# An embedding projection as split float32r products, and the last head's transposes two units later

## The chip, the cores and the metric

The kernel runs on one core of a Trainium2 chip. The metric is the device time of one execution, in microseconds (us), as the median of several runs. TensorE is called PE, with its weight loads as PEld; VectorE is DVE, ScalarE is ACT, GpSimd is POOL, SyncE is SP. SP, ACT and POOL also issue transfers (DMAs), each in its own order.

## The reference

One step of a one-layer decoder, for 512 prompt rows and 64 sample rows (576 rows in all, here split into two halves of 288 columns). All inputs are float32.

```python
def finish_layer(x, attn, conv_y, pe, g_attn_out, w_out, g_mlp, w_up, w_down, g_ple, w_ple, w_ple_gate):
    B, L = x.shape[0], x.shape[1]
    attn = rms_norm(attn, g_attn_out.reshape(N_HEADS, HEAD_DIM)).reshape(B, L, ATT_WIDTH)
    x = x + jnp.concatenate([attn, conv_y], axis=-1) @ w_out
    hid = jnp.square(jax.nn.relu(rms_norm(x, g_mlp) @ w_up))
    x = x + hid @ w_down
    gate = jax.nn.sigmoid(rms_norm(x, g_ple) @ w_ple_gate)
    return x + (pe @ w_ple) * gate
```

Ahead of this stand the input projection (q, k, v, forget gates and the convolution's inputs), attention of the prompt rows over themselves, attention of the sample rows over a paged cache of 2048 rows, and a causal convolution. The change concerns `pe @ w_ple`: `pe` is 576 x 256, `w_ple` 256 x 2048.

## The kernel before, in words

Everything is kept transposed: features lie on the 128 partitions, the 576 rows along the free dimension. A matmul's weights are a 128x128 block, its moving operand 288 columns.

Most products are made in three parts. A float32 operand is split into a high part of type float32r (ACT, `split_hi`, a copy that rounds) and the low rest (DVE, `split_lo`, operand minus high part). The product is then high x high + high x low + low x high. `mm6` issues this for one 128x128 block of weights: three parts for each of two halves of the rows, six matmuls into one accumulator `U` of PSUM. There are two accumulators U, and the tile allocator decides which one a new tile gets.

Phase 1 runs the input projection tile by tile (`gemm_tile`), and `half` is called between half chunks of it. There it takes one step each from queues of generators: convolution and the end of sample attention (`side`), the prompt heads (`att`, `prompt_head`), sample attention (`decode`). Each engine carries out its instructions in the order in which the program issues them.

When sample attention is through, the pool `mid` is opened, and `ple_loads` issues the loads of `pe` (tile `praw`) and of the first weights of `w_ple` (tile `wple`) from POOL. When the input projection is through, a loop drains the rest: per round two units of the embedding projection (`ple`), each followed by one step of the last prompt head, then one step of what is left of sample attention (`fq`), and one step of `out_rows`, which loads a pair of 128-row blocks of the attention result (`rp<-am`, from SP) and splits it into `xh[j]`, `xl[j]` for the output projection. Pairs 0 to 5 are built in the rounds; pairs 6 and 7, which hold the last heads, are loaded after all units and multiplied last in each tile of the output projection (`OUT_ORDER`).

A unit of `ple` makes 128 of the 2048 output features: plain float32 matmuls for two blocks of weights and two halves of rows, into one U. ACT (even units) or DVE (odd units) copies U into the tile `plt`, and SP stores it to `pl` in HBM, two units to a store. The weights come in four pieces of 512 KB, with two buffers, `praw` has a buffer of its own.

A step of the prompt head is: scores of a block of 128 queries, transposes of the probabilities (`turned`), product with the values (`values`). After the last `values`, a chain of twelve small DVE operations (`rsqrt`) normalizes the head's output `o`, PE transposes `o` (four transposes into `T`), ACT copies `T` to `amt`, and POOL stores it to `am`. While the input projection runs, two empty steps stand ahead of those transposes; during the drain there are none:

```python
        if not self.draining:
            for _ in range(2):
                yield
```

The units of the drain are numbered 0 to 15 here. Phase 2 (output projection's end, MLP, gate, final norm) follows behind and is not touched.

Of the kernel before, what the change touches and what calls it, by code (L numbers as in the profile page):

```python
# [9 lines left out]
F32 = mybir.dt.float32  # L10
F32R = mybir.dt.float32r
I32 = mybir.dt.int32
AF = mybir.ActivationFunctionType
# [132 lines left out]
class Kern:  # L146
# [102 lines left out]
    def phase1(self):  # L249
# [105 lines left out]
        nc.gpsimd.memset(f(self.cb), 0.0)  # L355


        side, att, fq = deque(), deque(), deque()
# [98 lines left out]
        assert D["mid"] is not None  # L457
        self.draining = True
        fq.extend(side)
        ple = self.ple(D["mid"])  # L460
        rows = self.out_rows(D["mid"])
        next(rows)
# [260 lines left out]
    def prompt_head(self, h, hb):  # L723
# [64 lines left out]
        for qt in range(4):  # L788
# [9 lines left out]
                self.rsqrt(sm, rs, ss, [128, 4], "h")  # L798
                nc.vector.tensor_tensor(o, o, rs[:, :, None].broadcast_to([128, 4, 128]), ALU.mult)
            yield  # L800
        if not self.draining:
            for _ in range(2):
                yield
        t = self.T_()
        for qt in range(4):
            nc.tensor.transpose(t[:, qt * 128:qt * 128 + 128], o[:, qt, :], self.ident)
# [304 lines left out]


    def ple_loads(self, mid):
        nc, a = self.nc, self.a
        self.pp = mid.tile([128, 2, NR], F32, name="praw", tag="p", bufs=1)
        nc.gpsimd.dma_start(self.pp, a["p"])
        self.wple = {}
        for e in range(2):
            self.ple_weights(mid, e)

    def ple_weights(self, mid, e):
        if e < 4:
            self.wple[e] = mid.tile([128, 8, 128], F32, name="wple", tag="wple")
            self.nc.gpsimd.dma_start(self.wple[e], self.a["w_ple"][e])

    def ple(self, mid):
        nc = self.nc
        for e in range(8):
            pr = mid.tile([128, 2, NR], F32, name="plt", tag="plt")
            w = self.wple[e // 2]  # L1130
            for n in range(2):
                u = self.U_()
                for kt in range(2):
                    for r in range(2):
                        nc.tensor.matmul(u[:, r, :HR], w[:, 4 * (e % 2) + 2 * n + kt, :], self.pp[:, kt, r * HR:(r + 1) * HR],
                                         start=(kt == 0), stop=(kt == 1))
                out = pr[:, n, :].rearrange("p (a b) -> p a b", a=2)
                if n:
                    nc.vector.tensor_copy(out, u[:, :, :HR])
                    nc.sync.dma_start(self.pl[e], pr)  # L1140
                    if e % 2:
                        self.ple_weights(mid, e // 2 + 2)
                else:
                    nc.scalar.activation(out, u[:, :, :HR], AF.Copy)
                yield


    def out_rows(self, mid):
# [737 lines left out]
def layout(inp):  # L1886
# [17 lines left out]
    d["w_ple"] = C(g["w_ple"][0].reshape(2, 128, 4, 4, 128).transpose(2, 1, 3, 0, 4).reshape(4, 128, 8, 128))  # L1904
# [56 lines left out]
```

## Time and profile before

| | |
|---|---|
| median of 3 runs | 2700.09 us (2697.12, 2700.09, 2708.5) |
| profiled execution | 2699.89 us |
| its span | 2698.1 us |
| granted clock of PE, mean | 0.996 |
| drain, first unit to first product of the output projection | 769.42 to 810.69 us |
| PE busy in the span | 98% |

The span is what the trace covers; the execution's own time is 1.8 us longer. In the rows of the trace a plain float32 matmul of the program shows as two records, a float32r matmul as one. A row in order of time gives its start, its length, engine, line, operation, what is written from what, the number of merged instructions, and in brackets the idle time of the engine just before with what ended it.

### The profile page before, as it was taken

Reading aid. Unit: us, or ns where it says so; the run is one execution under the profiler, and the core shown is the slowest. Engines: PE = TensorE matmul, PEld = TensorE weight load, DVE = VectorE, ACT = ScalarE, POOL = GpSimd, SP = SyncE. Lnnn points to the kernel's source line nnn. Section 1 sums busy time; section 2 is a strip of 40 time slices with the busy share of each in tenths; the row PEclk is TensorE's granted clock in tenths of the full one; section 3 lists DMA queues with packets and bytes.
Section 4 is the critical chain, followed back from the end, with each engine's and each line's share of the span. In section 5 each row is a group of like instructions: output and inputs, shape, how many; then the busy total and the mean of one; then the engine's idle time right before and its main releaser. Section 6 shows DMA issues by size and latency. Waiting matters only on the chain. (4 is left out here: it accounts for less than half of the span.)

```text
span 2698.1 us, 56355 instructions
## 1 busy us (share of the span) xinstructions
PE 2648.6 (98%) x21873; PEld 2561.3 (95%) x21873; DVE 2044.6 (76%) x3557; ACT 1160.0 (43%) x1704; POOL 517.3 (19%) x915
## 2 busy tenths in 40 slices
PE   9999999999999999999999999999999999999997
PEld 8899989888989999999999999999999999999997
DVE  6577777656554458888988888798888888888676
ACT  5222232335443335445544444454444444444554
POOL 2288786711000000001100000110000000000110
PEclk9999999999999999999999999999999999999999
DMA  5598888899755554445544444676565655656575
GB/s 204 174 303 295 292 295 289 294 308 321 260 191 162 173 195 161 156 142 165 165 144 141 138 146 142 237 204 186 166 186 153 182 163 172 181 174 219 185 240 168
DMA packets 240110, 544.38 MB, mean 202 GB/s; under 512 B 25729, under 2 KB 26754, under 8 KB 239842
## 3 DMA queue, kind: packets, MB, share of 16 engines
q1 hardware_dynamic: 171410, 330.95, 38.2%
q0 software_dynamic: 34896, 148.86, 17.4%
q10 hardware_dynamic: 33536, 60.96, 6.9%
q8 instruction: 171, 2.80, 0.4%
q14 instruction: 97, 0.79, 0.1%
HBM read 445.60 MB, written 95.09 MB: 200 GB/s over the span
## 5 line engine op out<-in xcount | busy, mean ns | idle before, releaser
L1607 PE MATMUL P<-xs,w2h 128*128 128x288 f32 x3584 | 1062.9, 297 | 8.1 <-DVE c L1726 3.8
L1608 PE MATMUL P<-xs,w2h 128*128 128x288 f32 x3584 | 1061.5, 296 | 2.0 <-DVE xs L155 2.0
L1609 PE MATMUL P<-xs,w2l 128*128 128x288 f32 x3584 | 1058.5, 295 | 2.5 <-DVE w2l L155 2.5
L152 ACT ACTIVATE w2h<-w2r 128x896 fp32r<-128x896 f32 (+1 forms) x632 | 560.3, 891 | 773.2 <-PE P L1608 459.1
L155 DVE TENSOR_TENSOR w2l<-w2r,w2h 128x896 fp32r<-128x896 f32 (+1 forms) x632 | 638.3, 1012 | 217.6 <-ACT w2h L152 215.5
L1607 PEld LDWEIGHTS P<-xs,w2h 128*128 128x128 f32 x3584 | 675.2, 188 | 14.1 <-DVE c L1726 7.0
L1608 PEld LDWEIGHTS P<-xs,w2h 128*128 128x128 f32 x3584 | 675.8, 189 | 3.4 <-DVE xs L155 3.2
L1609 PEld LDWEIGHTS P<-xs,w2l 128*128 128x128 f32 x3584 | 673.8, 188 | 3.9 <-DVE w2l L155 3.9
L498 PE MATMUL U<-xh,whi 128*128 128x288 f32 x1792 | 397.7, 303 | 0.1
L498 PE MATMUL U<-xl,whi 128*128 128x288 f32 x1792 | 381.4, 294 | 0.9 <-DVE xl L337 0.9
L498 PE MATMUL U<-xh,wlo 128*128 128x288 f32 x1792 | 381.7, 294 | 0.0
L498 PEld LDWEIGHTS U<-xh,whi 128*128 128x128 f32 x1792 | 285.9, 188 | 18.8 <-issue 16.3
L126 ACT ACTIVATE whi<-wraw 128x512 fp32r<-128x512 f32 x224 | 140.7, 629 | 355.1 <-PE U L498 295.2
L498 PEld LDWEIGHTS U<-xl,whi 128*128 128x128 f32 x1792 | 287.0, 188 | 1.8 <-DVE xl L337 1.7
L498 PEld LDWEIGHTS U<-xh,wlo 128*128 128x128 f32 x1792 | 286.9, 188 | 0.0
L132 DVE TENSOR_TENSOR wlo<-wraw,whi 128x512 fp32r<-128x512 f32 x224 | 158.3, 708 | 115.0 <-ACT whi L126 114.4
L1045 DVE SCALAR_TENSOR_TENSOR y<-ue,cv,y 128x512 f32<-128x512 f32 x240 | 184.7, 769 | 5.3
L1832 DVE TENSOR_TENSOR w2r<-w2r 128x512 f32<-128x512 f32 (+1 forms) x273 | 178.0, 652 | 5.1 <-DMA w2r<-in_w_down 5.1
L1046 POOL TENSOR_SCALAR cvt<-us,cv 128x64 f32<-128x64 f32 x240 | 165.4, 689 | 22.3
L1679 PE MATMUL P<-xs,w2l 128*128 128x288 f32 x512 | 151.6, 296 | 1.0 <-DVE w2l L155 0.9
L1677 PE MATMUL P<-xs,w2h 128*128 128x288 f32 x512 | 152.0, 297 | 0.0
L1678 PE MATMUL P<-xs,w2h 128*128 128x288 f32 x512 | 151.4, 296 | 0.0
(390 smaller groups left out, 2772.5 us busy)
## 6 DMA issues: line engine op xcount, KB each, us to landing
k<-in_cache_kv SPq DMA_DIRECT2D x256, 256.0 KB, 4.7
v<-in_cache_kv SPq DMA_DIRECT2D x256, 256.0 KB, 4.9
w2r<-in_w_up SPq DMA_DIRECT2D x127, 512.0 KB, 4.0
w2r<-in_w_down SPq DMA_DIRECT2D x112, 512.0 KB, 4.2
wraw<-in_w_main ACTq DMA_DIRECT2D x156, 256.0 KB, 5.0
xs<-di POOLq DMA_DIRECT2D x32, 1008.0 KB, 6.1
w2r<-in_w_gate SPq DMA_DIRECT2D x60, 512.0 KB, 4.5
x<-c POOLq DMA_DIRECT2D x48, 576.0 KB, 6.0
```

The source lines that it names most:

```text
L132: self.nc.vector.tensor_tensor(lo, self.raw.pop(c), f(hi), ALU.subtract)
L152: self.nc.scalar.activation(out, in_, AF.Copy, **kw)
L155: self.nc.vector.tensor_tensor(out, in_, f(hi), ALU.subtract)
L498: self.nc.tensor.matmul(u[:, r, :HR], w, x[:, r * HR:(r + 1) * HR], start=first and n == 0, stop=last and n == 2)
L1045: nc.vector.scalar_tensor_tensor(y, ue[:, j:j + NPR], w, y, ALU.mult, ALU.add)
L1046: nc.gpsimd.tensor_scalar(t, us[:, :, j:j + 8], w, None, ALU.mult)
L1607: nc.tensor.matmul(o, hi[:, ia, :], s.hi[:, ib, :], start=(i == 0), stop=False)
L1608: nc.tensor.matmul(o, hi[:, ia, :], s.lo[:, ib, :], start=False, stop=False)
L1609: nc.tensor.matmul(o, lo[:, ia, :], s.hi[:, ib, :], start=False, stop=(i == n - 1))
L1677: nc.tensor.matmul(o, hi[:, ia, :], s.hi[:, kh, rows], start=first and kh == 0, stop=False)
L1679: nc.tensor.matmul(o, lo[:, ia, :], s.hi[:, kh, rows], start=False, stop=last and kh == 1)
L1832: lambda: V(w[:, :, 4:6, :], w[:, :, 0:1, :].broadcast_to([128, m, 2, 128]), w[:, :, 1:3, :], ALU.add),
```

## The change

The embedding projection is made of split products. The input `praw` is split once into `px` (high and low). The weights come in eight pieces of 256 KB with three buffers, and are split unit by unit into `wph` (ACT) and `wpl` (DVE), two units ahead of their products. Input and the first two units are split by `ple_ahead`, a generator that `half` steps before the drain. `praw` now takes one of the two buffers of `rp`. Each unit has a `plt` of its own (three buffers) and its own store of 288 KB. The two empty steps ahead of the last head's transposes are now taken during the drain also.

```diff
+            step(pq)
...
+                    pq.append(self.ple_ahead(D["mid"]))
...
-        if not self.draining:
-            for _ in range(2):
-                yield
+        for _ in range(2 if self.draining else 2):
+            yield
...
+        self.praw = mid.tile([128, 2, NR], F32, name="praw", tag="rp")
+        self.nc.gpsimd.dma_start(self.praw, self.a["p"])
+        self.pl_x = mid.tile([128, 2, 2, NR], F32R, name="px", tag="px", bufs=1)
+        self.wple, self.units = {}, {}
+        for e in range(3):
             self.ple_weights(mid, e)
 
     def ple_weights(self, mid, e):
-        if e < 4:
-            self.wple[e] = mid.tile([128, 8, 128], F32, name="wple", tag="wple")
+        if e < 8:
+            self.wple[e] = mid.tile([128, 4, 128], F32, name="wple", tag="wple", bufs=3)
             self.nc.gpsimd.dma_start(self.wple[e], self.a["w_ple"][e])
+
+    def ple_unit(self, mid, u):
+        if u < 16:
+            e, n = u // 2, u % 2
+            hi, lo = (mid.tile([128, 2, 128], F32R, name=x, tag=x, bufs=3) for x in ("wph", "wpl"))
+            w = self.wple[e][:, 2 * n:2 * n + 2, :]
+            self.split_hi(hi, w)
+            self.split_lo(lo, w, hi)
+            self.units[u] = hi, lo
+            if n:
+                self.ple_weights(mid, e + 3)
+
+    def ple_ahead(self, mid):
+        for _ in range(4):
+            yield
+        for kt in range(2):
+            hi, lo, x = self.pl_x[:, 0, kt, :], self.pl_x[:, 1, kt, :], self.praw[:, kt, :]
+            self.split_hi(hi, x)
+            self.split_lo(lo, x, hi)
+            yield
+        for u in range(2):
+            self.ple_unit(mid, u)
+            yield
 
     def ple(self, mid):
         nc = self.nc
-        for e in range(8):
-            pr = mid.tile([128, 2, NR], F32, name="plt", tag="plt")
-            w = self.wple[e // 2]
-            for n in range(2):
-                u = self.U_()
-                for kt in range(2):
-                    for r in range(2):
-                        nc.tensor.matmul(u[:, r, :HR], w[:, 4 * (e % 2) + 2 * n + kt, :], self.pp[:, kt, r * HR:(r + 1) * HR],
-                                         start=(kt == 0), stop=(kt == 1))
...
+        xh, xl = self.pl_x[:, 0], self.pl_x[:, 1]
+        for i in range(16):
+            u = self.U_()
+            self.ple_unit(mid, i + 2)
+            hi, lo = self.units.pop(i)
+            for kt in range(2):
+                self.mm6(u, hi[:, kt, :], lo[:, kt, :], xh[:, kt, :], xl[:, kt, :], kt == 0, kt == 1)
+            t = mid.tile([128, NR], F32, name="plt", tag="plt", bufs=3)
+            out = t.rearrange("p (a b) -> p a b", a=2)
+            if i % 2:
+                nc.vector.tensor_copy(out, u[:, :, :HR])
+            else:
+                nc.scalar.activation(out, u[:, :, :HR], AF.Copy)
+            nc.sync.dma_start(self.pl[i // 2][:, i % 2, :], t)
+            yield
```

How the change stands in the engines' order is seen best at the end of the drain. PE before, from the head's last values (`S<-vn,pT`) over unit 11, the transposes (`T<-ident,o`) and units 12 to 15 to the output projection:

```order
L758 MATMUL S<-vn,pT 128x128 x4
L1135 MATMUL U<-praw,wple 128x288 x4
L806 MATMUL T<-ident,o 128x128 x4
L1135 MATMUL U<-praw,wple 128x288 x16
L498 MATMUL U<-xh_195,whi 128x288 x2
```

PE now, from the end of unit 12 (`U_12155`) over unit 13 (`U_12175`) and the transposes to the start of unit 14 (`U_12205`), with the engines whose signals an instruction waits for:

```order
L502 MATMUL U_12155<-px_11486,wpl_12093 128x288 x2
L502 MATMUL U_12175<-px_11486,wph_12134 128x288 [waits Activation_49]
L502 MATMUL U_12175<-px_11486,wph_12134 128x288 x3
L502 MATMUL U_12175<-px_11486,wpl_12135 128x288 [waits DVE_49]
L502 MATMUL U_12175<-px_11486,wpl_12135 128x288
L502 MATMUL U_12175<-px_11486,wph_12134 128x288 x4
L502 MATMUL U_12175<-px_11486,wpl_12135 128x288 x2
L809 MATMUL T_12195<-ident_156,o_11690 128x128 x4
L502 MATMUL U_12205<-px_11486,wph_12156 128x288 [waits DVE_49]
```

The transposes have moved behind units 12 and 13; they wait for nothing of their own any more, and unit 13 ahead of them waits for ACT at its first product and for DVE at its first product with `wpl`.

ACT before, from the split of row pair 3 (`xh_201`) over the copy of unit 10, the head's last output `o` with its squares, and the copy of the transposes (`amt`), to the copies of units 12 and 14 and pair 5:

```order
L152 ACTIVATE xh_201<-rp 128x1152
L1144 ACTIVATE plt<-U 128x576
L761 ACTIVATE o<-S,l_11686 128x128
L762 ACTIVATE S,ss<-S,l_11686 128x128
L808 ACTIVATE amt<-T,gat 128x512
L152 ACTIVATE xh_203<-rp 128x1152
L1144 ACTIVATE plt<-U 128x576 x2
L152 ACTIVATE xh_205<-rp 128x1152
```

ACT now, from the same split on:

```order
L152 ACTIVATE xh_201<-rp 128x1152
L152 ACTIVATE wph<-wple 128x256
L1166 ACTIVATE plt<-U 128x576
L765 ACTIVATE o<-S,l_11691 128x128
L766 ACTIVATE S,ss<-S,l_11691 128x128
L152 ACTIVATE wph<-wple 128x256
L152 ACTIVATE xh_203<-rp 128x1152
L152 ACTIVATE wph<-wple 128x256
L1166 ACTIVATE plt<-U 128x576
L152 ACTIVATE wph<-wple 128x256
L811 ACTIVATE amt<-T,gat 128x512
L152 ACTIVATE xh_205<-rp 128x1152
```

The split of pair 4 (`xh_203`) and two weight splits now stand ahead of the copy of unit 12, and the copy of the transposes stands behind them all; the copy of unit 14 follows behind pair 5.

DVE now, around the end of the chain that makes `o`: the low parts of the weights and the copies of units 11 and 13 stand behind it.

```order
L155 TENSOR_TENSOR wpl_12093<-wple_11928,wph_12092 128x256 [waits DMASW7_49,Activation_49]
L800 TENSOR_SCALAR ss_11692<-ss_11692 128x4 [waits Activation_49]
...
L803 TENSOR_TENSOR o_11690<-o_11690,rs_12119 128x512 [waits DVE_49]
L155 TENSOR_TENSOR wpl_12135<-wple_11928,wph_12134 128x256 [waits PE_49,Activation_49]
L1164 COPY plt_12150<-U_12133 128x576 [waits DMAHW3_49,DMAHW0_49,PE_49]
L155 TENSOR_TENSOR xl4_204<-rp_12029,xh4_203 128x1152 [waits DMAHW7_49,Activation_49]
```

Before, the copy of unit 11 stood right behind `o` there and no `wpl` existed. From the output projection on, every engine's order is the one before.

More of the change, by code (lines that the diff above doesn't have):

```diff
@@ L355, in phase1 @@
         nc.gpsimd.memset(f(self.cb), 0.0)
-        side, att, fq = deque(), deque(), deque()
+        side, att, fq, pq = deque(), deque(), deque(), deque()
         D = {"credit": 0.0, "dec": None, "mid": None, "rate": 0.0}
@@ L459, in phase1 @@
         fq.extend(side)
+        while step(pq):
+            pass
         ple = self.ple(D["mid"])
@@ L1113, in ple_loads @@
     def ple_loads(self, mid):
[L1114 to L1118, printed above, removed]
+        self.praw = mid.tile([128, 2, NR], F32, name="praw", tag="rp")
[3 more added lines that the diff above has]
+        for e in range(3):
@@ L1126, in ple @@
+    def ple_ahead(self, mid):
[9 more added lines that the diff above has]
+            yield
     def ple(self, mid):
         nc = self.nc
-        for e in range(8):
-            pr = mid.tile([128, 2, NR], F32, name="plt", tag="plt")
-            w = self.wple[e // 2]
-            for n in range(2):
-                u = self.U_()
-                for kt in range(2):
-                    for r in range(2):
-                        nc.tensor.matmul(u[:, r, :HR], w[:, 4 * (e % 2) + 2 * n + kt, :], self.pp[:, kt, r * HR:(r + 1) * HR],
-                                         start=(kt == 0), stop=(kt == 1))
[L1137 to L1145, printed above, removed]
@@ L1902, in layout @@
     d["w_gate"] = quads(g["w_ple_gate"][0], 8, 8)
-    d["w_ple"] = C(g["w_ple"][0].reshape(2, 128, 4, 4, 128).transpose(2, 1, 3, 0, 4).reshape(4, 128, 8, 128))
+    d["w_ple"] = C(g["w_ple"][0].reshape(2, 128, 8, 2, 128).transpose(2, 1, 3, 0, 4).reshape(8, 128, 4, 128))
     ck = g["cache_k"][0].transpose(0, 3, 2, 1).reshape(-1, 128, 2, 4, 128)
```

## The prediction, made before the result was known

> **What bounds the kernel now.** I read the page's busy shares first, then the busy time by stretch around the changed stage, then the order in time of that stage's instructions, and last the landing times of its transfers.
>
> ```profile
> span 2698.1 us, 56355 instructions
> PE 2648.6 (98%) x21873; PEld 2561.3 (95%) x21873; DVE 2044.6 (76%) x3557; ACT 1160.0 (43%) x1704; POOL 517.3 (19%) x915
> PEclk9999999999999999999999999999999999999999
> ...
> 769.00:790.00 21.00, 20.61 (x107) 15.71 (x106) 10.97 (x33) 10.60 (x27) 1.09 (x2) 1.00 0.41 152
> 790.00:811.00 21.00, 18.89 (x92) 14.98 (x91) 9.75 (x21) 10.42 (x21) 1.20 (x3) 1.00 0.72 246
> 811.00:836.00 25.00, 25.00 (x193) 25.00 (x192) 10.77 (x13) 7.09 (x10) 0.00 (x0) 1.00 0.57 186
> ```
>
> PE is busy 98% of the span at full clock, and after 811 us nothing interrupts it: what is gained or lost before 811 us moves the end by the same amount. The columns after each stretch are its length and the busy time of PE, weight loads, DVE, ACT, POOL. From 769 to 811 us PE lacks 2.5 us, and DVE and ACT are half idle. This is the stage that the change rewrites.
>
> ```profile
> 765.98 0.43 PE L498 MATMUL U<-xh,wlo 128*128 128x288 f32 x2
> ...
> 769.42 4.04 PE L1135 MATMUL U<-praw,wple 128*128 128x288 f32 x16
> ...
> 774.74 0.62 PE L978 MATMUL D<-v_s,fpT 64*32 64x128 f32 x10 [0.39 <-ACT v_s L784]
> ...
> 795.60 2.11 PE L1135 MATMUL U<-praw,wple 128*128 128x288 f32 x8
> 797.54 1.05 PE L758 MATMUL S<-vn,pT 128*128 128x128 f32 x8
> 798.43 2.11 PE L1135 MATMUL U<-praw,wple 128*128 128x288 f32 x8
> 802.65 0.66 PE L806 MATMUL T<-ident,o 128*128 128x128 f32 x4 [2.11 <-DVE o L799]
> 803.14 7.93 PE L1135 MATMUL U<-praw,wple 128*128 128x288 f32 x32
> 810.69 0.64 PE L498 MATMUL U<-xh,whi 128*128 128x288 f32 x2
> ...
> 812.50 0.43 PE L498 MATMUL U<-xh,whi 128*128 128x288 f32 x2
> ...
> 815.70 0.43 PE L498 MATMUL U<-xh,whi 128*128 128x288 f32 x2
> ```
>
> The two waits in brackets are the 2.5 us. One of 2.11 us stands ahead of the last head's four transposes, which need o from DVE; the other, 0.39 us, waits for v_s and is not touched.
>
> **The products.** A unit of the projection (I number them 0 to 15) is now 8 records of PE (x8), and 795.60 to 797.54 makes it 1.94 us. The split unit is twelve float32r products of 288 columns, the form of the output projection's rows: from 812.50 to 815.70 there are 24 of them, 0.133 us each, so a unit takes 1.60 us. Gain 0.34 us a unit, 16 units: **-5.4 us**. Bounds: 0.133 us comes from the same shape and weight pattern, so I allow 0.32 to 0.36 us a unit, 5.1 to 5.8 us.
>
> The Trainium skill, page "FP8 and Floating Point Precision", section "TensorE Precision Notes", says that a true fp32 product takes four passes through the array; with three passes for the split form the old unit would be four thirds of 1.60, an estimate of 2.13 us, and the gain 8.5 us. The rows disagree with that price (1.94 us), and the sum goes by the rows.
>
> **The old wait.** Two units now stand between the last values and the transposes in addition to the one before, 3.2 us of work against a wait of 2.11 us: **-2.1 us**. What is late next is below, since these units have waits of their own.
>
> **The splits.** Each unit now needs a high part on ACT and a low part on DVE, 128x256, and the input needs two pairs of 128x576.
>
> ```profile
> L752 ACT ACTIVATE pT<-T 128x256 f32<-128x256 f32 x1 | 0.4, 383 | 1.5 <-PE T L750 1.5
> L982 DVE TENSOR_TENSOR fon<-fon,foc 128x256 f32<-128x256 f32 x1 | 0.4, 425 | 0.0
> L1144 ACT ACTIVATE plt<-U 128x576 f32<-128x576 f32 x8 | 5.2, 651 | 5.9 <-PE U L1135 4.9 <-ACT p L744 0.6 <-DMA pl<-plt 0.5
> L1139 DVE COPY plt<-U 128x576 f32<-128x576 f32 x8 | 6.1, 757 | 13.3 <-PE U L1135 13.3
> L152 ACT ACTIVATE xh<-rp 128x1152 fp32r<-128x1152 f32 x8 | 9.3, 1161 | 0.6 <-DMA rp<-am 0.6
> L155 DVE TENSOR_TENSOR xl<-rp,xh 128x1152 fp32r<-128x1152 f32 x8 | 10.9, 1357 | 5.5 <-ACT xh L152 5.5
> L808 ACT ACTIVATE amt<-T,gat 128x512 f32<-128x512 f32 x2 | 1.4, 687 | 3.9 <-PE T L806 3.9
> ```
>
> ACT: 16 x 0.38 and 2 x 0.65 = 7.4 us; DVE: 16 x 0.42 and 2 x 0.76 = 8.3 us, spread over some 45 us in which each is half idle. As a total that is hidden. A unit is split two units ahead of its products, 3.2 us at least for a chain of 0.8 us. The input's parts fall before 769 us:
>
> ```profile
> 763.52 1.28 DVE L132 TENSOR_TENSOR wlo<-wraw,whi 128x512 fp32r<-128x512 f32 x2
> ...
> 792.71 1.36 DVE L155 TENSOR_TENSOR xl<-rp,xh 128x1152 fp32r<-128x1152 f32 x1 [1.29 <-ACT xh L152]
> ...
> 801.91 0.69 DVE L799 TENSOR_TENSOR o<-o,rs 128x512 f32<-128x512 f32 x1
> ...
> 820.81 1.36 DVE L155 TENSOR_TENSOR xl<-rp,xh 128x1152 fp32r<-128x1152 f32 x1 [0.19 <-ACT xh L152]
> ```
>
> The first px low part goes between the two wlo of 763.52 and makes the second end at 765.6 in place of 764.8; PE multiplies with that chunk's wlo at 765.98, so 0.4 us of slack is left. I cost it at 0, at most 0.4.
>
> **What waits in their place.** The pieces of work that lie in order on ACT and DVE decide the end of the stage. Their transfers:
>
> ```profile
> rp<-am SPq DMA_DIRECT2D x8, 576.0 KB, 5.7
> pl<-plt SPq DMA_DIRECT2D x8, 576.0 KB, 3.9
> ...
> wple<-in_w_ple POOLq DMA_DIRECT2D x4, 512.0 KB, 7.6
> ...
> am<-amt POOLq DMA_DIRECT2D x2, 256.0 KB, 2.8
> ...
> DMA to landing us min/median/max: 3.9/5.7/6.6
> ...
> DMA to landing us min/median/max: 2.8/3.9/6.7
> ...
> DMA to landing us min/median/max: 4.8/7.6/9.2
> ...
> 805.29 0.65 ACT L1144 ACTIVATE plt<-U 128x576 f32<-128x576 f32 x1 [0.20 <-PE U L1135]
> ...
> 794.10 0.32 SPq L1154 DMA_DIRECT2D rp<-am  x1
> ...
> 812.35 1.29 SPq L1154 DMA_DIRECT2D rp<-am  x2
> ```
>
> The three lines of min/median/max are those of rp, pl and wple.
>
> Unit 11 starts at 798.43 now; 11 x 0.34 earlier is 794.7. Units 11 and 12 take it to 797.9, where unit 13 would start. But the order of the changed program shows unit 13 waiting for ACT: its accumulator is not the one of unit 11 (whose copy stands on DVE behind the 4 us of o) but that of unit 12 (the allocator gives both the same PSUM banks), so it needs ACT's copy of unit 12. At best that copy starts 0.2 us after unit 12 (now at 805.29, where 803.14 + 1.94 = 805.08 ends unit 12) and takes 0.65: a wait of 0.9 us. Ahead of it on ACT stand the high part of row pair 4 (1.16 us) and a weight split (0.38). Pair 4 is loaded when the low part of pair 2 is done: 794.07 now, about eight units' gain earlier then, 791.4. With rp's median of 5.7 us it lands at 797.1, the high part ends at 798.3, the split at 798.6, the copy at 799.25: unit 13 starts at 799.3, a wait of **+1.4 us**. With a landing of 6.6 us it is 2.3; with 3.9 us the floor of 0.9. I take 1.4, the median landing. Unit 13's own low part stands on DVE behind o; o ends 4.2 us after 798.43 now, so about 4.2 to 4.7 after 794.7, and the low part is there by 799.8, while PE needs it 0.53 us into the unit: covered.
>
> After the transposes, units 14 and 15 and the first tile of the output projection depend on DVE's low parts behind a row split of 1.36 us, and on ACT's copy of unit 14, which stands behind amt (0.69) and the high part of pair 5 (1.16). With the transposes at 801.0 these end near 804.2, PE reaches the output projection at 804.6. I put +0.5 us there, between 0 (all covered) and 1.3 (landings at their slowest).
>
> SP: sixteen stores of half the size in place of eight, the same bytes; its queue shows 0.3 us an issue, 2.6 us more in 40 us, free. POOL: eight loads in place of four; a load goes out five units before its first split, 11 us at 2.2 us a unit with the attention work between, against 9.2 us for the slowest load twice the size: free. The second row load now waits until the input is split, near 767 us, and is first used in the third round, 14 us later, against 6.6 us for the slowest landing: free.
>
> The transposes are also late for those who wait for them: amt, its store (2.8 us), and the load of the last row pair, which the first output tile multiplies last. Now four units (7.6 us) stand between the transposes and the output projection, then two (3.2 us). But that last load is issued behind the last store of the projection, at 812.35 to 813.2, 1.7 us and more after the output projection begins at 810.69. Then: transposes end, 0.2 + 0.69 + 0.2 + 2.8 = 3.9 us later the row has landed, 0.7 us after the two units' 3.2 us, and the last store is still what the load waits for. So 0. There is no reserve further on: pair 7's low part ends at 820.81 + 1.36 = 822.17, 11.5 us after 810.69, and the first tile's last two of 16 steps begin 11.2 us after it. Every us by which that load is later is a us of the end.
>
> **Sum.** -5.4 - 2.1 + 1.4 + 0.5 = -5.6 us against the profiled execution's 2699.89 us (span 2698.1 and 1.8 around it): 2694.3. The median of the three runs stands 0.2 us above that execution; I take **2694.5**.
>
> **Rivals.** (1) The waits are covered: allocation and landings favour PE and only the 0.9 us floor, or nothing, is left: -6.6 to -7.5 us, 2692.4 to 2693.3. For it: rp's shortest landing, 3.9. Against it: pair 4 is one of the slow ones now (below, issue at 794.1).
>
> ```profile
> rp<-am SPq DMA_DIRECT2D x1, 576.0 KB, 6.6
> ```
>
> (2) The row loads stay at 6.6 us and the stage crams the same bytes into less time: units 12 and 13 wait 2.3 + 0.4, the last pair 0.9 as well: -5.4 - 2.1 + 2.7 + 1.3 + 0.9 = -2.6, 2697.3. (3) Slower: the stores hold the units. plt has three half-size buffers, so a unit cannot follow the third before it faster than copy, issue and landing: (0.7 + 0.3 + L) / 3. A unit with all between it takes 41.3 / 16 = 2.58 us now; break-even is L = 6.7, the longest store there is, and 9 us would give 3.3 us a unit, +12 us, 2712. Against it: the longest belongs to twice the size, and the median is 3.9. (4) The change takes no time off because the new wait equals the old: it would need 7.5 us of new waits, 3.6 times the old one; that is the edge of (2) and (3).
>
> On (3) the Trainium skill speaks for caution: page "DMA: Bandwidth & Descriptors", section on the anatomy of a DMA on the SWDGE path, puts about 2.0 us on each transfer whatever its size, so a halved store would land in an estimated 2.0 + 1.9 / 2 = 2.95 us and not in half of 3.9. No run here shows a store of that size from this queue.
>
> **How the numbers follow.** My forecast 0.5, (1) 0.15, (2) 0.27, (3) and (4) 0.08. The likeliest case alone spans 2693 to 2696. With (1) and (2), and a scatter of the runs before from 2697.12 to 2708.5, 0.1% below and 0.3% above their median, the range is 2690 to 2701. Half a per cent, about what a measurement of this kernel can tell from no change, is 13.5 us: no case of gain reaches it, since the whole stage offers 7.5; only a far end of (3) or a scatter of the runs would pass it on the other side. Faster 0.03, within 0.94, slower 0.03.
>
> **What would show it.** A unit of twelve products at 1.60 us; no wait ahead of the transposes; a wait of 1 to 2 us ahead of unit 13 with ACT's plt as its releaser; the first output-projection product near 804 to 806 us in place of 810.7; the rest of the span unchanged in length. I am wrong if units wait for a wpl or a store in the middle of the stage, if the first output tile stands before its last steps, or if the phases behind it change their own length.

## The result, and the profile after

| | before | after |
|---|---|---|
| median, 6 executions each | 2701.99 us (2697.12 to 2708.5) | 2693.09 us (2688.96 to 2701.05) |
| ratio, 95% interval | | 0.9964 (0.995 to 0.9978) |
| profiled execution / its span | 2699.89 / 2698.1 us | 2701.05 / 2699.3 us |
| first unit to first product of the output projection | 41.27 us | 35.81 us |
| that product to the sum of the first output tile | 13.14 us | 15.07 us |
| sum of the first to sum of the 16th output tile | 187.2 us | 192.0 us |
| from there to the end of the span | 1687.1 us | 1687.3 us |

The changed kernel is 0.2 to 0.5% faster, within the half per cent of the prediction. The execution that was profiled is the slowest of its six, so its span is longer than before; the last three lines of the table say where. The drain is 5.5 us shorter, 1.9 us are given back in the first output tile, and 4.8 us in the fifteen tiles behind it, which the change does not touch.

The drain's end on PE after (units 12 and 13, the transposes, the start of the output projection, and the two stops in its first tile):

```profile
796.11 0.69 PE L502 MATMUL U<-px,wph 128*128 128x288 f32 x4
796.64 0.42 PE L502 MATMUL U<-px,wpl 128*128 128x288 f32 x2
796.90 0.69 PE L502 MATMUL U<-px,wph 128*128 128x288 f32 x4
...
799.42 0.80 PE L502 MATMUL U<-px,wph 128*128 128x288 f32 x4 [1.56 <-ACT plt L1166]
...
801.12 0.60 PE L809 MATMUL T<-ident,o 128*128 128x128 f32 x4
...
804.88 0.43 PE L502 MATMUL U<-xh,whi 128*128 128x288 f32 x2
...
815.33 0.53 PE L502 MATMUL U<-xh,whi 128*128 128x288 f32 x2 [0.70 <-ACT xh L152]
816.73 0.53 PE L502 MATMUL U<-xl,whi 128*128 128x288 f32 x2 [0.86 <-DVE xl L155]
```

Six products take 0.79 us (796.11 to 796.90), a unit 1.6. The transposes wait for nothing. The new waits are those of unit 13, and of pair 6's high and low part in the first output tile. ACT in the same stretch shows what stood behind both, landings of row loads:

```profile
797.16 1.17 ACT L152 ACTIVATE xh<-rp 128x1152 fp32r<-128x1152 f32 x1 [1.28 <-DMA rp<-am]
798.72 0.65 ACT L1166 ACTIVATE plt<-U 128x576 f32<-128x576 f32 x1
801.76 0.69 ACT L811 ACTIVATE amt<-T,gat 128x512 f32<-128x512 f32 x1 [2.08 <-PE T L809]
...
814.11 1.17 ACT L152 ACTIVATE xh<-rp 128x1152 fp32r<-128x1152 f32 x1 [2.29 <-DMA rp<-am]
815.73 1.16 ACT L152 ACTIVATE xh<-rp 128x1152 fp32r<-128x1152 f32 x1 [0.45 <-DMA rp<-am]
```

The transfers issued at the drain's end, with the mean rate over the stretch and the median from issue to landing, after (795 to 816 us):

```profile
DMA packets 2841, 5.82 MB, mean 277 GB/s; under 512 B 814, under 2 KB 814, under 8 KB 2840
...
rp<-am SPq DMA_DIRECT2D x3, 576.0 KB, 5.4
pl<-plt SPq DMA_DIRECT2D x6, 288.0 KB, 4.4
wraw<-in_w_out ACTq DMA_DIRECT2D x4, 256.0 KB, 5.0
...
am<-amt POOLq DMA_DIRECT2D x1, 256.0 KB, 7.8
```

and before, in the same stage of the program (801 to 820 us):

```profile
am<-amt POOLq DMA_DIRECT2D x1, 256.0 KB, 2.6
```

The load of pair 6, for which PE stops now, was issued at 812.35 in the kernel before (at 806.29 now), and ACT's split of it began 5.7 us later (7.8 now):

```profile
818.06 1.17 ACT L152 ACTIVATE xh<-rp 128x1152 fp32r<-128x1152 f32 x1 [0.19 <-DMA rp<-am]
```

The 4.8 us behind the first tile show in the sums of the output tiles, first and last start, before:

```profile
L1179 DVE TENSOR_TENSOR c<-U,rx x16: 757/758/758, 823.8 to 1011.0; 128x576 f32<-128x576 f32 x16
```

and after:

```profile
L1202 DVE TENSOR_TENSOR c<-U,rx x16: 756/756/757, 820.0 to 1012.0; 128x576 f32<-128x576 f32 x16
```

A tile took 12.48 us before and 12.80 after. PE had no idle time there in either; its products simply come 0.130 us apart in the one and 0.133 in the other, as the count in a stretch of full work shows, before:

```profile
850.00:1000.00 150.00, 150.00 (x1156) 150.00 (x1155) 68.85 (x107) 46.86 (x70) 11.36 (x21) 1.00 0.53 175
```

and after:

```profile
850.00:1000.00 150.00, 150.00 (x1127) 150.00 (x1126) 65.66 (x104) 46.11 (x68) 11.37 (x21) 1.00 0.51 172
1330.00:1730.00 400.00, 400.00 (x3002) 400.00 (x3002) 343.94 (x539) 187.00 (x215) 32.18 (x60) 1.00 0.46 147
```

So three questions stood at the start of the experiments: is that pace due to the change, what is each part of the change worth, and whose wait is the one ahead of unit 13 and the ones in the first output tile.

### The profile page after: what moved, and what is told of

It reads as the page before. It is cut to its first block, busy times and chain, and to the rows that moved or that the text cites. A ratio compares the mean times of both kernels' runs of the same rounds, so it can differ in the third digit from the quotient of the medians.

```text
span 2699.3 us, 56554 instructions
## 1 busy us (share of the span) xinstructions
PE 2651.0 (98%) x21937; PEld 2569.4 (95%) x21937; DVE 2050.9 (76%) x3575; ACT 1165.4 (43%) x1722; POOL 519.3 (19%) x919
```

## The experiments

One row for each profile. The columns count from the drain's first unit, since the stages ahead of it, which these kernels hardly change, ended anywhere from 766.7 to 775.2 us.

| kernel | first unit to output projection | to the first tile's sum | together | last tile's sum to the end | median of all executions, ratio |
|---|---|---|---|---|---|
| before | 41.27 | 13.14 | 54.4 | 1687.1 | |
| before, again | 43.16 | 13.93 | 57.1 | 1682.0 | |
| delay alone | 39.95 | 13.67 | 53.6 | 1685.0 | 2702.27, 0.9999 (0.9985 to 1.0012) |
| after | 35.81 | 15.07 | 50.9 | 1687.3 | 2693.09, 0.9964 (0.995 to 0.9978) |
| after, again | 36.08 | 14.37 | 50.4 | 1686.9 | 2695.88, 0.9976 (0.9964 to 0.9989) |
| split products alone | 37.07 | 14.67 | 51.7 | 1678.6 | 2699.47, 0.9992 (0.9981 to 1.0003) |
| pair 6 early | 36.06 | 17.97 | 54.0 | 1678.5 | 2696.81, 0.9984 (0.9971 to 0.9997) |
| pair 4 late | 35.76 | 14.45 | 50.2 | 1681.9 | |
| stores late | 36.33 | 15.38 | 51.7 | 1687.8 | 2696.55, 0.9976 (0.9963 to 0.999) |
| both late | 35.56 | 16.24 | 51.8 | 1681.8 | 2695.49, 0.9977 (0.9964 to 0.999) |
| am from ACT | 36.32 | 14.09 | 50.4 | 1686.9 | |
| four plt buffers | 38.04 | 15.04 | 53.1 | 1676.5 | |
| all of them | 36.43 | 12.99 | 49.4 | 1682.8 | 2693.49, 0.9973 (0.9957 to 0.9988) |
| am and last stores from ACT | 36.20 | 12.99 | 49.2 | 1685.8 | 2694.37, 0.9964 (0.995 to 0.9978) |

### The pace: both kernels once more

No edit.

> The changed kernel once more, to separate what the change does from what an execution does. In the two profiles so far the changed kernel ends its first output tile 3.9 us earlier (sum of that tile starts at 819.95 against 823.84 us), but ends its last output tile 1.0 us later (1012.0 against 1011.0), because PE takes 0.1333 us a product there against 0.1300 before. Theory A (pace by execution): the step from 820 to 1012 us and the long stretches behind it run at one of two or three paces (0.130, 0.132, 0.133 us a product of 288 columns) that an execution falls into by chance. Then this profile ends its first output tile at 819.5 to 820.5 us again, has stretches whose pace differs from the first profile of the same kernel, and the median of the ratios is 0.995 to 0.999 with executions spread over 8 us or more. Theory B (pace by kernel): the change itself puts the output projection at 0.1333; then every stretch has the pace it had in the first profile, within 0.0003 us.

> The kernel before once more, for its pace. Its first profile ran the output projection's tiles 2 to 16 at 0.130 us a product (12.48 us a tile); the five profiles of other kernels ran them at 0.1333 (12.80 us a tile). Theory A (an execution falls into a pace by chance): this profile may show 12.80 us a tile as well, and long stretches between 1070 and 2420 us will differ in pace from those of the first profile. Theory B (0.130 belongs to the plain products): tile sums again 12.48 us apart.

Measured, for the changed kernel: the drain and the first tile repeat (50.4 us against 50.9), and the output tiles come 12.80 us apart again. Its long stretches keep their pace too, but for 3070 products from 1890 to 2300 us in place of 3082; alone it would hardly have decided between the theories. The kernel before decides: its tiles, too, now come 12.80 us apart and not 12.48.

```profile
L1179 DVE TENSOR_TENSOR c<-U,rx x16: 758/758/758, 825.5 to 1017.5; 128x576 f32<-128x576 f32 x16
```

The same program thus ran these tiles at 0.130 once and at 0.133 us a product once; of the fourteen profiles only the first shows 0.130 from tile to tile. The stretches behind differ likewise. From 1330 to 1730 us four of the profiles have 3038 or 3039 products, as split products alone has, and the other ten have 3002 or 3003:

```profile
1330.00:1730.00 400.00, 400.00 (x3038) 400.00 (x3038) 348.77 (x547) 191.66 (x221) 33.96 (x63) 1.00 0.47 151
```

36 products are 4.8 us. These four also have the four shortest ways from the last output tile to the end (1676.5 to 1681.8 us, the other ten 1681.9 to 1687.8 us), though the kernels do not differ there. The clock does not sort them: its mean over the span is 0.994 to 0.996 in the four and 0.993 to 0.996 in the other ten. Theory A holds in the main: the way from the last tile's sum to the end differs by up to 11 us between profiles, most of it with the pace of PE, and a change of 5 us is seen in a profile only where its own stage is compared. What sets the pace stays open; the granted clock is 1.00 in all these rows.

The second profile of the kernel before has 1.9 us more in its drain than the first. Its waits there are the same two, 0.39 and 2.31 us; the column behind POOL's shows a stretch of lower clock:

```profile
790.00:812.00 22.00, 19.69 (x87) 15.31 (x86) 9.35 (x21) 10.53 (x21) 1.07 (x3) 0.92 0.70 235
```

0.08 of 22 us is 1.8 us. The drain proper is therefore 41.3 us before and 35.8 to 36.1 after.

### The parts alone

The split products without the delay:

```diff
-        for _ in range(2 if self.draining else 2):
+        for _ in range(0 if self.draining else 2):
```

> The changed kernel with the last head's transposes where they were (no empty steps in the drain), so split products and small pieces alone. Theory A (each wait is where its own chain ends): products 1.60 us a unit, a wait of about 2.8 us ahead of the transposes (o is ready at 798.9, unit 11 ends at 796.1), no wait ahead of unit 13, the first product of the output projection at 805.7 to 806.2 against 804.9 with the delay: the two steps are worth about 1 us and not 2.1, since unit 13's wait of 1.56 us took their place. am's store goes out by 800.5 and lands in 3 to 4 us, pair 6's load still stands behind the last store at about 807.3. The first output tile ends 0 to 2 us later than with the delay. Rival (the delay costs more than it brings, because am's late store crowds the row loads of pairs 6 and 7): the stall in the first output tile (1.56 us) is gone and the tile ends at the same time or earlier, 819.0 to 820.0.

Measured: 37.07 us to the output projection (805.83), and the wait is back at its old place, longer than before, since the units around it are shorter:

```profile
798.86 0.66 PE L809 MATMUL T<-ident,o 128*128 128x128 f32 x4 [2.67 <-DVE o L803]
```

Unit 13 waits for nothing. The delay is worth 1.0 to 1.3 us and not the 2.67 us of the wait that it removes: 1.5 of them stand ahead of unit 13 instead. The early store of am goes out at 801.8, ahead of the weight loads of 804.4, and lands fast:

```profile
am<-amt POOLq DMA_DIRECT2D x1, 256.0 KB, 2.5
```

Yet the first tile still stops, 0.86 us for pair 6's low part, since the row loads go out behind the last store at 807.3. So the rival, that the late am costs more than the delay brings, falls.

The delay with the plain products:

```diff
-        if not self.draining:
-            for _ in range(2):
-                yield
+        for _ in range(2):
+            yield
```

> The kernel before with the two empty steps ahead of the last head's transposes also in the drain; products plain fp32 as before. Theory A: the wait of 2.11 us ahead of the transposes goes; unit 13 now waits for DVE's copy of unit 11, which stands behind o (o ends at 802.6, copy at 803.3, unit 12 ends at 802.3), so about 1.0 us comes back: the output projection starts at 809.4 to 809.9 against 810.69, a gain of 0.8 to 1.3 us. Rival (the delay is free): 808.6, a gain of the whole 2.1 us. In the total time neither can be seen: ratio 0.998 to 1.001.

Measured: 39.95 us to the output projection, 1.3 us less than before, the upper end of theory A; 0.74 us of the 2.11 come back ahead of unit 13 as a wait for DVE's copy:

```profile
808.42 2.21 PE L1134 MATMUL U<-praw,wple 128*128 128x288 f32 x8 [0.74 <-DVE plt L1138]
```

The two parts together, from the first unit to the output projection: 41.27 less 4.2 (split products) less 1.3 (delay) is 35.8, the changed kernel. They add up.

### The first output tile

Pair 6's load ahead of the last stores:

```diff
-            if j < 4:
+            if j < 5:
                 load(j + 2)
             yield
-        load(6)
         load(7)
```

> The changed kernel with the load of row pair 6 (it needs no late head) issued when pair 4 is split, in place of behind the last store of the projection. Theory A: the stall of 0.70 + 0.86 us in the first output tile is pair 6's load, issued at 806.29 behind the last store and landing 7.8 us later among six other transfers; issued at about 801.2 it lands before 808 and the stall goes: first output tile ends 1.3 to 1.8 us earlier, sum of the tile at 818.2 to 818.7. Rival (pair 7 is the late one, through am's store that now goes out at 804.0 and lands at 811.8): the stall stays at 1 us or more, with the split of pair 7 as its releaser.

Theory A falls. The stop moved to pair 7 and grew, from 1.56 to 3.35 us:

```profile
820.13 0.53 PE L502 MATMUL U<-xh,whi 128*128 128x288 f32 x2 [2.49 <-ACT xh L152]
821.52 0.78 PE L502 MATMUL U<-xl,whi 128*128 128x288 f32 x2 [0.86 <-DVE xl L155]
```

With pair 6's 576 KB out first, DVE's copy of unit 15 waited for a store to free its plt buffer (DVE, same profile), so the last store went out at 810.3, and pair 7's load at 812.9, when am's store, 7.7 us under way, had landed:

```profile
809.55 0.76 DVE L1164 COPY plt<-U 128x576 f32<-128x576 f32 x1 [3.44 <-DMA pl<-plt]
```

The last three stores behind the row loads, still from SP:

```diff
-            nc.sync.dma_start(self.pl[i // 2][:, i % 2, :], t)
+            store = lambda i=i, t=t: nc.sync.dma_start(self.pl[i // 2][:, i % 2, :], t)
+            if i < 13:
+                store()
+            else:
+                self.last_stores.append(store)
...
         for _ in rows:
             pass
+        for store in self.last_stores:
+            store()
         mes.close()
```

> The changed kernel with the last three stores of the projection (units 13, 14, 15: 0.86 MB) issued behind the loads of row pairs 6 and 7. Theory (the drain's end is a pile-up of transfers: from 803 to 813 us seven transfers at about 400 GB/s, so that am's store lands after 7 to 7.8 us in place of 2.6, and pair 7's load, which waits for it, with it): with three stores fewer am's store lands within 5.5 us, pair 7's load is out by 809 and lands by 814.5; the first tile's waits fall from 1.2 to 1.6 us to 0.6 us or less, its sum comes 13.2 to 13.9 us after the first product of the output projection (15.1, 14.4 and, with pair 6 early, 18.0 so far). Rival (queueing on SP, not the transfers' number, delays the row loads): am's store still takes 7 us, since pair 6's load now goes out beside it, pair 7 lands at 818 and the first tile waits 3 us as with pair 6 early.

The rival came: am's store took 6.4 us all the same (7.8 and 7.0 in the changed kernel's profiles), pair 7's load went out at 814.1 with three stores on its heels and landed 6 us later. Waits of 0.60 and 0.86 us remain in the tile. The 400 GB/s of the expectation were too high: from 803 to 813 us the changed kernel moved 259 GB/s on average.

am's last store from ACT instead of POOL:

```diff
-        nc.gpsimd.dma_start(self.am[h // 2][:, h % 2, :NPR], am)
+        (nc.scalar if self.draining else nc.gpsimd).dma_start(self.am[h // 2][:, h % 2, :NPR], am)
```

> The changed kernel with the last head's store to am issued by ACT right behind amt, in place of by POOL. In every profile with split products POOL issues it 1.54 us after amt's end (0.29 us in those with plain products), 0.2 to 0.6 us behind two weight loads of the output projection, and it lands 6.4 to 7.8 us later; alone, at 801.8 in the kernel with the early transposes, it took 2.5 us. Theory (the store is slow because it goes out behind the two weight loads): from ACT it is out ahead of them, about 0.1 to 0.4 us after amt's end, and lands in 3 to 4.5 us, so pair 7's load goes out right behind pair 6's; the first tile's wait shrinks to pair 6's share, 0.5 to 1.0 us. Rival (the transfers share the engines whatever the order): it lands in 6 us or more all the same, and the first tile's sum stays 14.4 to 15.1 us behind the first product.

Now it is out 0.03 us behind amt's end and ahead of the weight loads (ACT's queue), and pair 7's load follows pair 6's at once, at 809.8, so that it landed within 5.4 us; the first tile waits 0.49 us for pair 6 and 0.12 for pair 7. ACT, then PE:

```profile
804.39 0.33 ACTq L812 DMA_DIRECT2D am<-amt  x1
...
806.10 0.85 ACTq L115 DMA_DIRECT2D wraw<-in_w_out  x2
```

```profile
818.39 0.54 PE L502 MATMUL U<-xl,whi 128*128 128x288 f32 x2 [0.49 <-DVE xl L155]
```

So pair 7's load went out 0.44 us behind pair 6's and not 5.5 us as in the changed kernel, which speaks for the theory; the store's exact landing is not in the trace. In time this edit alone shows nothing: 50.4 us to the first tile's sum, as in one of the changed kernel's two profiles.

### The wait ahead of unit 13

Row pair 4 split behind unit 12's copy (`n` is the round; units 12 and 13 are round 7):

```diff
             next(ple, None)
+            if n == 7:
+                next(rows)
             step(att)
...
-            if 1 < n < 8:
+            if 1 < n < 8 and n != 6:
                 next(rows)
```

> The changed kernel with row pair 4 split behind unit 12's copy in place of ahead of it. Theory (unit 13 waits for ACT's copy of unit 12, and that stands behind pair 4, which lands late): the copy starts 0.2 us after unit 12 ends, unit 13's wait falls from 1.46 to 1.56 us to 0.8 to 1.0 us, still with ACT's plt as its releaser; transposes 0.6 us earlier after the first unit (31.4 in place of 31.9 to 32.1 us). Rival (another wait is right behind, DVE's low part of unit 13's weights behind o): the wait moves to the first product with wpl and unit 13 ends when it did. The first output tile gains nothing or loses, since its end hangs on the row loads: first product of the output projection 35.0 to 35.5 us after the first unit (35.8 and 36.1 now), first tile's end as before.

PE after this edit, and ACT:

```profile
805.18 0.80 PE L504 MATMUL U<-px,wph 128*128 128x288 f32 x4 [1.18 <-ACT plt L1168]
```

```profile
804.48 0.65 ACT L1168 ACTIVATE plt<-U 128x576 f32<-128x576 f32 x1 [1.89 <-DMA pl<-plt]
```

The releaser is the copy, as the theory has it, but 1.18 us are left: with pair 4 away, the copy waits for a store to free one of three plt buffers. Two causes stood one behind the other.

The size alone would not show that pair 4 counts. In six profiles whose order up to unit 13 is the changed kernel's, the wait is 0.94 to 1.56 us, and 1.18 lies inside. These six speak for the theory by another row: where pair 4's load landed in 5.40 and 5.67 us (am from ACT, stores late), unit 13 waited 0.94 and 1.03 us, and where it took 5.85 to 6.06 us (after, after again, pair 6 early), 1.46 to 1.56; in the sixth its landing is not in the trace.

Both edits (pair 4 late, stores late):

> Both: pair 4 behind unit 12's copy, and the last three stores behind the row loads. Theory: the two gains add, since unit 13's wait and the first tile's wait have different causes: first unit to first product 35.0 to 35.5 us, first product to first tile's sum 13.2 to 14.2 us, together 1.5 to 2.5 us less than the changed kernel's 50.4 to 50.9 us. In the total time 0.05 to 0.1%, within the scatter: ratio to the kernel before 0.996 to 0.999. Rival (the earlier start of the output projection meets the same row loads and waits for them): first tile's sum 50 us after the first unit, as now.

The sum came 51.8 us after the first unit, as the rival has it, but not for the rival's reason. Unit 13 waited 1.58 us, ACT's copy 2.29 us for a store, and PE stopped in the first tile for 0.28 and 0.86 us. PE then began the second tile 50.0 us after the first unit, against 50.7 and 50.3 in the changed kernel. Only DVE's sum was late: the load of the rows that it adds (`rx`) now stands behind the three stores on SP and goes out at 814.75.

```profile
820.55 0.76 DVE L1211 TENSOR_TENSOR c<-U,rx 128x576 f32<-128x576 f32 x1 [2.68 <-DMA rx<-in_x]
```

So in this row of the table "together" overstates what PE lost, by 1.6 us, and in the row "stores late", where the sum waited 1.50 us for `rx`, by 0.4. In the other rows the sum follows the second tile's first product by 0.2 us.

A fourth plt buffer, at the price of one of the three buffers of weights, with pair 4 late:

```diff
-            self.wple[e] = mid.tile([128, 4, 128], F32, name="wple", tag="wple", bufs=3)
+            self.wple[e] = mid.tile([128, 4, 128], F32, name="wple", tag="wple", bufs=2)
...
-            t = mid.tile([128, NR], F32, name="plt", tag="plt", bufs=3)
+            t = mid.tile([128, NR], F32, name="plt", tag="plt", bufs=4)
```

> Pair 4 behind unit 12's copy, and four plt buffers in place of three (the weights of the projection then have two buffers in place of three, for room). With three, unit 12's copy waited 1.89 and 2.29 us for a store to land once pair 4 no longer stood ahead of it, and unit 13 waited 1.18 and 1.58 us. Theory (two causes one behind the other, pair 4's landing and then the third buffer's store): with both away only the copy itself is left, and unit 13 waits 0.8 to 1.0 us; no copy on ACT or DVE waits for pl over 0.3 us. Rival (the weights' loads with two buffers hold the splits): a wait for wple of 0.5 us or more appears on ACT, and a unit waits for wph or wpl.

The rival again, by the split of unit 14's weights, which stands ahead of the copy of unit 12 (PE, then ACT):

```profile
797.86 1.29 PE L504 MATMUL U<-px,wph 128*128 128x288 f32 x4 [2.50 <-ACT plt L1168]
```

```profile
796.85 0.42 ACT L152 ACTIVATE wph<-wple 128x256 fp32r<-128x256 f32 x1 [3.37 <-DVE wpl L155]
```

The row names DVE's low part of unit 13, which ends at 796.76; the load of unit 14's weights landed at 796.74. With two buffers these weights come too late in any case, and the copy of unit 12 stands behind their split. That a fourth buffer alone would bring the wait to the copy's 0.9 us could not be shown, for want of room.

### The version with the freed first tile

All edits, with the last three stores issued by ACT behind the split of pair 7:

> All that the experiments point to: pair 4 behind unit 12's copy, four plt buffers, am's last store from ACT, and the last three stores of the projection issued by ACT behind the split of pair 7, where nothing waits for them. Theory: first unit to first product of the output projection 34.8 to 35.4 us (35.8 and 36.1 in the changed kernel), first product to the first tile's sum 13.3 to 13.9 us (14.4 and 15.1), together 48.2 to 49.2 us against 50.5 and 50.9. In the total time that is 0.06 to 0.1%: ratio to the kernel before 0.995 to 0.998. Rival (each wait removed uncovers the next transfer): 50 us or more from the first unit to the first tile's sum.

and without the two that cost more than they brought (four plt buffers, pair 4 late):

```diff
-        nc.gpsimd.dma_start(self.am[h // 2][:, h % 2, :NPR], am)
+        (nc.scalar if self.draining else nc.gpsimd).dma_start(self.am[h // 2][:, h % 2, :NPR], am)
...
-            nc.sync.dma_start(self.pl[i // 2][:, i % 2, :], t)
+            def store(q, i=i, t=t):
+                q.dma_start(self.pl[i // 2][:, i % 2, :], t)
+            if i < 13:
+                store(nc.sync)
+            else:
+                self.last_stores.append(store)
...
         for _ in rows:
             pass
+        for store in self.last_stores:
+            store(nc.scalar)
         mes.close()
```

> The changed kernel with only the two edits that freed the first output tile: am's last store from ACT behind amt, and the projection's last three stores from ACT behind the split of pair 7; weights and plt with three buffers each, pair 4 where it was. Theory (the wait ahead of unit 13 and the waits in the first output tile are separate, and two buffers of weights cost 2.3 to 3.4 us in the last two kernels): first unit to first product of the output projection 35.5 to 36.4 us as in the changed kernel, first product to the first tile's sum 13.0 to 13.4 us (13.0 is 96 products at 0.1333 and 0.2), together 48.6 to 49.6 us. Rival (with weights loaded early the drain is fuller, and the row loads land late again): the first tile waits 1 us or more and its sum stays 50 us or more behind the first unit. In the total time: ratio 0.996 to 0.998, not to be told from the changed kernel's.

In both the first tile runs without a stop, 12.99 us (96 products of 0.1333 us and 0.19 to the sum). The first has a drain of 36.43 us instead of 35, since unit 13 waits 2.45 us for the weights' reason above; the second fulfils its expectation, 36.20 and 49.2 us, with 1.32 us left ahead of unit 13 and 0.41 ahead of unit 15. The two edits free the tile together: in the second kernel pair 6's load goes out at 799.76, 4 us ahead of the output projection, and pair 7's at 806.0. Its stage is 1.2 to 1.7 us better than in the changed kernel. In the total time, 2694.37 us against 2693.09 and 2695.88, that cannot be told; both beat the kernel before.

## Why the prediction was right, and where it was not

The time, 2694.5 us, lies between the changed kernel's two medians, 2693.09 and 2695.88. By its steps:

- **The products, -5.4.** Right: 0.79 us for six, 1.6 a unit against 1.94. Between marks with the same kinds of products on both sides (the scores ahead of unit 0, at 768.94 and 768.78, and the second pair of products of the output projection, at 811.17 and 805.15) the stage is 42.23 us before and 36.37 after, 5.9 less. The waits ahead of the transposes and of unit 13, 2.11 and 1.56 us, account for 0.55 of it, so the sixteen units gave 5.3. The 8.5 us estimated from four passes a product (the Trainium skill, "FP8 and Floating Point Precision", "TensorE Precision Notes") do not agree with these rows.
- **The old wait, -2.1.** Gone, as said.
- **Unit 13, +1.4.** Right to 0.2: 1.56 and 1.46 us, unit 13 at 799.42 (799.3 was forecast), for the reason given. What the step did not see is the second cause behind the first: the third plt buffer's store. It was priced only as an all-or-nothing rival, (3), with a break-even at a landing of 6.7 us; in fact single copies waited for stores at landings of 4.5 us median, on DVE for 1.61 us at 793.54 in the changed kernel, covered there.
- **Units 14 and 15, +0.5.** Too much for the first profile, where neither waits; unit 15 waits 0.32 us in the second, and up to 0.82 in the other kernels with this order. What unit 13 does not wait, unit 15 partly does: the two together wait 1.5 to 1.8 us in all six profiles, against a forecast of 1.9. The prediction names two arrivals at the output projection: 804.6 is the way through its chain without these 0.5 us, its sum gives 805.1; measured 804.88.
- **The splits, 0.** Right: 0.413 us on ACT and 0.421 on DVE, and no unit of the profiled changed kernel waited for a split of its weights.
- **The last row pairs, 0.** Wrong, the one step that failed. It followed pair 7 alone, through am's store, and put no wait on pair 6, whose load stands behind the last store as well and had no reserve either: before, its low part ended at 820.62 and the product that needs it began at 820.77. That load went out at 806.29 and was split from 814.11, 7.8 us later (7.0 in the second profile, 5.7 before), and PE stopped for its high and its low part. The first tile gave 1.2 to 1.9 us back. Pair 7 stood right behind: am's store was taken at 2.8 us, 0.2 us behind amt; it went out 1.54 us behind amt, beside two weight loads, and landed in 7.8. Pair 7's load therefore left at 811.82, and with pair 6 early the stop moved to pair 7. Rival (2) had this place with 0.9 us, for pair 7. Why the landings are longer is argued from their company, not shown: am's store took 2.5 to 2.6 us where it landed before the weight loads went out, 4.8 where they went out 1 us behind it (delay alone), and 6.4 to 7.8 beside or behind them; but pair 6's load took 7.2 us in the kernel with split products alone also, where am's store had long landed. That transfers of several engines interleave on the same sixteen DMA engines is in the Trainium skill ("DMA: Bandwidth & Descriptors", "Issuing engines are not separate DMA queues"); the landings of am's store agree with it.
- **Stores of half the size.** The fixed part of a transfer in the Trainium skill ("DMA: Bandwidth & Descriptors", anatomy of one DMA) had given an estimate of 2.95 us. That section is about transfers that GpSimd issues, and these go out from SP, so it was carried over. Measured are landings of 2.1, 4.5 and 6.4 us (shortest, median, longest) against 3.9 median at twice the size: half the size did not make them land sooner in this stage.
- **The rest unchanged in length.** Not so in the profiled pair, 4.8 us in fifteen tiles; but the change is not the cause, since the kernel before has the same 12.80 us a tile in its second profile.

The stage itself therefore gained 3.5 to 4.0 us against the first profile of before, and 4.4 to 4.9 against the second without its lower clock (57.1 - 1.8 less 50.9 or 50.4), where 5.6 was forecast. The measured gain of the medians is larger, 8.9 us and, against 2701.64, 5.8; by the intervals it is 5.9 to 13.5 and 3.0 to 9.7 us, which holds the stage's gain in the second comparison and not in the first. Whether a difference in the mix of paces is behind the rest cannot be said from two profiles of each. That 2694.5 came out so near is in part luck: the first tile's 1.2 to 1.9 us, missed, and what the stage does not explain lie on opposite sides.

## What to carry to other kernels

A wait that is covered by moving work ahead of it is worth what the next wait behind it leaves: here 1.0 to 1.3 us of 2.7. Where a stage is made shorter with the same bytes in it, cost every transfer at its end with the landings of a crowded stretch, the one with a dependent load behind it first, and issue that one ahead of loads that have time; two edits of places in the queues, am's store from ACT and the last three stores behind the row loads, freed the first tile together, and one that only moved a load earlier made it worse. Before a time is read from one engine's mark, as the sum of the first tile here, check that this engine waits for the work in question and not for a transfer of its own. And with a scatter like this one's, compare the stage from a mark inside it, not the spans.

## What the runs showed of the hardware

- The pace of one and the same product, 128x128 by 288 columns of float32r with PE never idle and a granted clock of 1.00, is 0.130, 0.1317 or 0.1333 us, each held for up to some hundred us, and it differs between executions of one program. The Trainium skill, "TensorE: Matmul & The Clock Gate", "Wait — 56ns, not 53.3ns?", puts a product at its columns by 2.4 GHz and 2.5 ns, an estimate of 122.5 ns here; none of the three paces is that.
- am's store left POOL 1.54 us behind amt's end in the changed kernel and 0.29 us in the kernel before, with the same wait for amt. In the first nothing stands ahead of it that waits for an earlier transfer, in the second a separate wait does; whether that is the cause was not tried.
